# Three engines' orders written by hand from the output projection on, in a one-layer mLSTM and attention encoder

## The chip, the cores and the metric

The kernel runs on one core of a Trainium2 chip. A core has engines that run beside each other and wait for one another through semaphores: TensorE (PE) multiplies matrices into PSUM, VectorE (DVE) and ScalarE (ACT) work elementwise, GpSimd (POOL) and SyncE (SP) here mostly issue DMAs. The metric is the device time of one execution in microseconds (us); lower is better. Times are medians of several executions; the profile is of one more.

## What is computed

One layer on a sequence of 512 rows of width 2048, all in float32, with two branches (an mLSTM and a differential attention), their gated mix, an output projection and a feed-forward block:

```python
def reference(x, ..., w_out, norm2_w, w_ffn_in, w_ffn_out, final_norm_w):
    ...                                   # branches, gates -> mix  (512 x 2048)
    x = x + mix @ w_out                   # output projection    "wo"
    h = _rmsnorm(x, norm2_w)
    u = h @ w_ffn_in                      # 2048 x 11264         "fi"
    x = x + gated(u) @ w_ffn_out          # 5632 x 2048          "fo"
    return _rmsnorm(x, final_norm_w)
```

The change touches what begins with `mix @ w_out`. (The last four lines are condensed; `gated` is the silu-gated half product of the feed-forward block.)

## The kernel before

**One product.** A float32 product is made of three passes with reduced operands: each operand is split into a high part and a rest, and `mm3` (L145) issues high x high, high x low and low x high. The high part is an ACT copy (`whi_...`, L149), the low part a DVE subtraction (`wlo_...`, L150). So each piece of weights (128x1024) costs ACT one copy and DVE one subtraction before TensorE can use it, and so does each piece of activations, called a factor here (`..h`, `..l`, two halves of 128x512).

**Seven instead of eight.** `seven` multiplies 2x2 blocks with seven products (Strassen's scheme in Winograd's form). Each product Q1, Q5, Q6, Q2, Q3, Q7, Q4 takes a sum of weight blocks and a sum of activation blocks. The sums of weights are DVE additions: raw_b += raw_a (L348), `t2` (L356), raw_e += raw_f (L362), `t2` += raw_d (L369). A chunk runs over groups g of 512 rows: Q1, Q5, Q6 for every group, then Q2, Q3, Q7, then Q4. A product of one group is twelve matmuls of 128x512. Names say all this: `wlo_fi4_Q12` is the low part of the weights of chunk fi4, product Q1, group 2. The last chunks, fo, also have four plain products, `W12`, `W22`, `W11`, `W21`.

**Chunks.** wo0 and wo1 (4 groups each), fi0 to fi10 (4 groups, 28 products each), fo0 and fo1 (10 groups and the plain ones). While a chunk runs, `post` takes finished PSUM banks into tiles: in wo and fo by `added` (L802 to L837: the residual is added by an accumulating DMA that POOL issues, the squares for the norm are ACT's), in fi by L938 to L956 (sigmoid on ACT, sums and gate on DVE).

**Between chunks.** `turned` transposes a finished block on TensorE (eight transposes of 128x128 make a set, `T`), ACT copies them out of PSUM (`fg_X`, `h_X`), and four DVE operations, `sum_` at L863 (S1, then X21, X11 and X12 in place), make the sums of activation blocks for later products; SP stores each sum, and ACT's queue stores the plain blocks. `h2c` are the blocks after wo (h20 and h21 from wo0), `fg_j` those after fi chunk j. They come back from DRAM as `fs` (L988, POOL's queue) and are split into factors while fo runs. A set of transposes of chunk j runs inside chunk j+1.

**What sets the order.** The code hands over instructions in the order in which it is written; a scheduler then orders each engine's own stream by priorities and by times that it estimates, and puts the waits in. `take` (L206) fetches the weight pieces of product n and has piece n+2 made (`AHEAD` = 2). `work` (L332) does one queued factor after each product; `later` (L213) puts a step off by a number of nanoseconds of a clock that counts matmuls. Each engine then runs its stream in order, and an instruction that waits holds what stands behind it on its engine.

## Time and profile before

| | us |
|---|---|
| median of 3 runs | 2681.12 (2680.89 to 2682.58) |
| the profiled execution | 2683.64 |
| its span | 2681.9 |
| TensorE busy in the span | 2605.4 (97%) |
| VectorE busy | 2129.2 (79%) |
| ScalarE busy | 1312.8 (49%) |

The span is the time from the first to the last instruction of the profiled execution; the time itself holds 1.74 us more around it. Shares of the whole span are means over stages. By the names in the timeline of TensorE, wo lasts from 1177.6 to 1358.2 us, fi to 2225.1, fo to 2670.9, and the end to 2681.9. The granted clock is a share of TensorE's full clock of 2.4 GHz, so 0.50 is its lower level, 1.2 GHz.

### The profile page before, as it was taken

To read this page: it belongs to the slowest core of one execution; us is meant where nothing else is said; L and a number is where in the kernel's file an instruction comes from. 1 tells how busy PE (TensorE), PEld (TensorE's weight loads), DVE (VectorE), ACT (ScalarE), POOL (GpSimd) and SP (SyncE) were. 2 spreads that over 40 slices of the span, in tenths; PEclk is the share of its full clock that TensorE was granted. 3 is DMA by queue.
4 is the path that set the end of the run, shared out by engine and by line. 5 is a ranking of instruction groups with operands and counts; after the bars stand their busy time and mean duration, and the time that the engine had idled before them with its cause. 6 is when DMAs were issued, how large, how long until landed. Compare 5 with 4: busy or idle time off the path is not lost.

```text
span 2681.9 us, 33178 instructions
## 1 busy us (share of the span) xinstructions
PE 2605.4 (97%) x12136; PEld 2160.3 (81%) x12136; DVE 2129.2 (79%) x2692; ACT 1312.8 (49%) x1848; POOL 254.9 (10%) x448
## 2 busy tenths in 40 slices
PE   8999999999999999999899999999999999999997
PEld 7888888877878998887778888888888878777876
DVE  8977788777877676596788888888888889888885
ACT  8544444444544463345464444444444446546654
POOL 1000000011110113101110000000000002222211
PEclk9999999989999999999999999999999999999999
DMA  7655666633432346437665555555555578777763
GB/s 263 233 186 185 201 200 216 223 103 116 123 110 71 115 134 241 175 130 233 223 199 183 194 165 181 195 192 186 175 199 173 181 284 286 252 249 257 242 220 94
DMA packets 162227, 508.97 MB, mean 190 GB/s; under 512 B 21832, under 2 KB 22120, under 8 KB 162064
## 3 DMA queue, kind: packets, MB, share of 16 engines
q1 hardware_dynamic: 111456, 379.77, 41.3%
q0 software_dynamic: 33712, 97.71, 12.1%
q10 hardware_dynamic: 16896, 29.37, 3.1%
q8 instruction: 95, 1.56, 0.2%
q14 instruction: 68, 0.56, 0.1%
HBM read 445.41 MB, written 50.87 MB: 185 GB/s over the span
## 4 chain that ended last, share of the span: by engine, by line
PE 71%; DVE 12%; issue 7%; DMA 7%; ACT 2%; POOL 1%; SPq 0%; DVEq 0%; POOLq 0%; ACTq 0%
PE fi_b L145 12%; PE fi_c L145 8%; PE fi_a L145 8%; PE fo_b L145 4%; PE aqk_b L145 3%; PE fo_c L145 3%; PE fo_a L145 3%; PE mqk_b L145 3%; PE mv_p L145 3%; PE ba_p L145 3%; PE bm_p L145 3%; PE ga_b L145 2%; PE gm_b L145 2%; PE gm_a L145 1%; PE gm_c L145 1%
## 5 line engine op out<-in xcount | busy, mean ns | idle before, releaser
L145 PE MATMUL aqk_b<-xs,whi_aqk 128*128 128x512 f32 x512 | 162.0, 396 | 0.0
L149 ACT CAST whi_fi_Q<-fi_Q_t 128x1024 fp32r<-128x1024 f32 x88 | 92.5, 1052 | 117.7 <-PE fi_b L145 97.7
L145 PE MATMUL fi_a<-whi_fi_Q,h_X 128*128 128x512 f32 x440 | 147.0, 391 | 0.0
L145 PE MATMUL fi_c<-whi_fi_Q,h_S 128*128 128x512 f32 x440 | 145.0, 390 | 0.0
L145 PE MATMUL fi_b<-whi_fi_Q,h_S 128*128 128x512 f32 x352 | 115.5, 389 | 0.0
L145 PEld LDWEIGHTS aqk_b<-xs,whi_aqk 128*128 128x128 f32 x512 | 97.1, 191 | 19.6
L150 DVE TENSOR_TENSOR wlo_fi_Q<-fi_Q_t,whi_fi_Q 128x1024 fp32r<-128x1024 f32 x88 | 106.5, 1220 | 5.5 <-ACT whi_fi_Q L149 5.3
L145 PE MATMUL aqk_b<-xs,wlo_aqk 128*128 128x512 f32 x256 | 100.8, 394 | 0.0
L145 PEld LDWEIGHTS fi_c<-whi_fi_Q,h_S 128*128 128x128 f32 x440 | 83.0, 189 | 17.3
L145 PEld LDWEIGHTS fi_a<-whi_fi_Q,h_X 128*128 128x128 f32 x440 | 82.6, 188 | 16.8
L362 DVE TENSOR_TENSOR raw_fi_e<-raw_fi_e,raw_fi_f 128x1024 f32<-128x1024 f32 x44 | 53.9, 1224 | 52.6 <-DMA raw_fi_e<-in_w_ffi 52.6
L988 POOL DMA_DIRECT2D fs_X<-fg_X11d x22 | 11.9, 539 | 830.5 <-DVE wlo_fi_Q L150 785.3
L145 PE MATMUL fi_a<-wlo_fi_Q,h_X 128*128 128x512 f32 x220 | 85.9, 390 | 0.6 <-DVE wlo_fi_Q L150 0.6
L145 PE MATMUL fi_c<-wlo_fi_Q,h_S 128*128 128x512 f32 x220 | 85.8, 390 | 0.0
L348 DVE TENSOR_TENSOR raw_fi_b<-raw_fi_b,raw_fi_a 128x1024 f32<-128x1024 f32 x44 | 53.8, 1224 | 36.0 <-DMA raw_fi_b<-in_w_ffi 33.6
L149 ACT CAST whi_fi_Q<-raw_fi_e 128x1024 fp32r<-128x1024 f32 x44 | 46.4, 1055 | 72.6 <-PE fi_b L145 51.4
L145 PE MATMUL ba_p<-whi_ba,hahl 128*128 128x512 f32 x256 | 81.8, 390 | 0.0
L145 PE MATMUL mqk_b<-xs,whi_mqk 128*128 128x512 f32 x256 | 80.9, 396 | 0.0
L145 PE MATMUL bm_p<-whi_bm,hmhl 128*128 128x512 f32 x256 | 80.5, 391 | 0.0
L149 ACT CAST whi_fi_Q<-raw_fi_b 128x1024 fp32r<-128x1024 f32 x44 | 46.5, 1057 | 68.8 <-PE fi_c L145 52.1
L149 ACT CAST whi_fi_Q<-raw_fi_f 128x1024 fp32r<-128x1024 f32 x44 | 46.5, 1056 | 68.3 <-PE fi_c L145 63.9
L145 PEld LDWEIGHTS fi_b<-whi_fi_Q,h_S 128*128 128x128 f32 x352 | 66.1, 188 | 13.7
(843 smaller groups left out, 8479.5 us busy)
## 6 DMA issues: line engine op xcount, KB each, us to landing
raw_fi_a<-in_w_ffi SPq DMA_DIRECT2D x44, 512.0 KB, 3.4
raw_fi_b<-in_w_ffi SPq DMA_DIRECT2D x44, 512.0 KB, 4.2
raw_fi_c<-in_w_ffi SPq DMA_DIRECT2D x44, 512.0 KB, 4.1
raw_fi_d<-in_w_ffi SPq DMA_DIRECT2D x44, 512.0 KB, 4.2
raw_fi_f<-in_w_ffi SPq DMA_DIRECT2D x44, 512.0 KB, 3.5
raw_fi_e<-in_w_ffi SPq DMA_DIRECT2D x44, 512.0 KB, 3.6
raw_aqk<-in_w_aqk SPq DMA_DIRECT2D x32, 512.0 KB, 3.5
raw_fo_a<-in_w_ffo SPq DMA_DIRECT2D x20, 512.0 KB, 4.5
```

Source lines behind the costliest of these rows:

```text
L145: T.matmul(dst, lhs[l], rhs[r], start=first and i == 0, stop=last and i == 2, skip_group_check=skip)
L149: A.copy(hi, src)
L150: V.tensor_tensor(lo, src, hi.bitcast(F32), ALU.subtract)
L348: V.tensor_tensor(raws[r12], raws[r12], raws[r11], ALU.add)
L362: V.tensor_tensor(raws[r12], raws[r12], raws[r22], ALU.add)
L988: G.dma_start(got[n], fgd[g][f_].rearrange("p (k c) -> p k c", k=2))
```

## The change

From the first product of wo0 on, `tc.manual_schedule()` is entered and never left: each engine then issues in the order in which the code is written, and the scheduler moves nothing. Along with it the code is written in another order:

- `parts` makes the high part of a weight piece at once, when `issue` comes to it, and hands back a function that makes the low part. `take(n)` has the high part of piece n+2 made as before, and calls the functions so that low parts up to piece n+1 are made.
- `post` of a finished product is not called behind that product but put off by 2000 ns (`behindhand`), that is about one product.
- `factor` makes the high part at once and puts the low part into a list; `work` takes one of the list each time. `flush` empties it before the two sums that change a tile whose low part is still to be made.
- The factors of fo are made only when fewer than five of those made are unused (`used`), instead of whenever `work` comes by.

```diff
@@ -174,9 +174,13 @@
...
-        lo = wpool.tile([P, n], F32R, tag="lo", name=f"wlo_{name}")
-        split(src, hi, lo)
-        return tuple(w.rearrange("p (k c) -> p k c", k=kt) for w in (hi, lo))
+        A.copy(hi, src)
+
+        def low():
+            lo = wpool.tile([P, n], F32R, tag="lo", name=f"wlo_{name}")
+            V.tensor_tensor(lo, src, hi.bitcast(F32), ALU.subtract)
+            return tuple(w.rearrange("p (k c) -> p k c", k=kt) for w in (hi, lo))
+        return low
...
@@ -197,6 +201,22 @@
+    region = []
+
+    def written():
+        if not region:
+            region.append(ctx.enter_context(tc.manual_schedule()))
+
+    def behindhand(fn):
+        if region:
+            later(2000, fn)
+        else:
+            fn()
+
+    lows = [0]
...
@@ -206,6 +226,9 @@
         issue(n + AHEAD)
+        while lows[0] < min(len(ready), n + (2 if region else 3)):
+            ready[lows[0]] = ready[lows[0]]()
+            lows[0] += 1
...
     def work(must=False):
+        if low_parts:
+            low_parts.pop(0)()
...
         def body(nm, it):
+            if nm == "wo0":
+                written()
...
+                used[0] += len({(g, f_) for _, f_ in to} - met)
+                met |= {(g, f_) for _, f_ in to}
...
-                    post(q_, bank)
+                    behindhand(lambda q_=q_: post(q_, bank))
...
@@ -457,8 +490,19 @@
-        split(src, *w)
-        out[f_] = w
+        A.copy(w[0], src)
+
+        def low():
+            V.tensor_tensor(w[1], src, w[0].bitcast(F32), ALU.subtract)
+            out[f_] = w
+        if region:
+            low_parts.append(low)
+        else:
+            low()
+
+    def flush():
+        while low_parts:
+            low_parts.pop(0)()
...
         def s2():
+            flush()
...
         def s4():
+            flush()
...
             if q_ == "Q4" and j == NFB - 1:
+                used[0] = -4
                 stream()
...
-        when(lambda: True, [lambda n=n: make(n) for n in range(len(need))])
+        for n in range(len(need)):
+            when(lambda n=n: n < used[0] + 5, [lambda n=n: make(n)])
```

Nothing is added or left out: on every engine the program holds the same instructions as before, and up to wo0 in the same order. Three places show the moves.

DVE, in chunk fi4. TensorE's products run Q10, Q50, Q60, Q11, Q51, Q61, Q12, Q52 and so on; a set of transposes for `fg3` stands in the middle of Q11 before the change. Before:

```order
L150 TENSOR_TENSOR wlo_fi4_Q61_14745<-fi4_Q61_t2_14742,whi_fi4_Q61_14744 128x1024
L863 TENSOR_TENSOR fg3_S1_14769<-fg3_X21_14759,fg3_X22_14766 128x512
L356 TENSOR_TENSOR fi4_Q63_t2_14880<-raw_fi4_b3_14721,raw_fi4_c3_14740 128x1024
L863 TENSOR_TENSOR fg3_X21_14759<-fg3_X11_14619,fg3_X21_14759 128x512
L150 TENSOR_TENSOR wlo_fi4_Q12_14787<-raw_fi4_a2_14630,whi_fi4_Q12_14786 128x1024
L863 TENSOR_TENSOR fg3_X11_14619<-fg3_S1_14769,fg3_X11_14619 128x512
L369 TENSOR_TENSOR fi4_Q60_t2_14685<-fi4_Q60_t2_14685,raw_fi4_d0_14784 128x1024
L863 TENSOR_TENSOR fg3_X12_14627<-fg3_X12_14627,fg3_X11_14619 128x512
```

After, at the same place; the set of transposes now stands in the middle of Q51:

```order
L181 TENSOR_TENSOR wlo_fi4_Q61_14764<-fi4_Q61_t2_14742,whi_fi4_Q61_14744 128x1024
L909 TENSOR_TENSOR fg3_S1_14787<-fg3_X21_14777,fg3_X22_14784 128x512
L909 TENSOR_TENSOR fg3_X21_14777<-fg3_X11_14637,fg3_X21_14777 128x512
L909 TENSOR_TENSOR fg3_X11_14637<-fg3_S1_14787,fg3_X11_14637 128x512
L909 TENSOR_TENSOR fg3_X12_14645<-fg3_X12_14645,fg3_X11_14637 128x512
L376 TENSOR_TENSOR raw_fi4_b2_14648<-raw_fi4_b2_14648,raw_fi4_a2_14614 128x1024
L181 TENSOR_TENSOR wlo_fi4_Q12_14807<-raw_fi4_a2_14614,whi_fi4_Q12_14762 128x1024
L384 TENSOR_TENSOR fi4_Q62_t2_14823<-raw_fi4_b2_14648,raw_fi4_c2_14673 128x1024
```

The four sums, which wait for the transposes, stand in one piece ahead of the addition and of `wlo` of Q12, where `wlo` of Q12 had two of them behind it. The addition to raw_b2, made much earlier before, stands between too. The same holds at fi1 to fi10, ten times.

DVE, from wo0 into wo1 (h21 and h20 are the blocks made of wo0's result; `wo0_x210` and `wo0_x211` are its last tiles). Before:

```order
L348 TENSOR_TENSOR raw_wo1_b2_11451<-raw_wo1_b2_11451,raw_wo1_a2_11410 128x1024
L150 TENSOR_TENSOR wlo_wo1_Q10_11413<-raw_wo1_a0_11194,whi_wo1_Q10_11412 128x1024
L150 TENSOR_TENSOR wlo_wo1_Q50_11455<-raw_wo1_b0_11213,whi_wo1_Q50_11454 128x1024
L837 TENSOR_TENSOR wo0_x210_11064<-wo0_x210_11064,wo0_b0_10807 128x512
L863 TENSOR_TENSOR h21_S1_11482<-h21_X21_11433,h21_X22_11441 128x512
L837 TENSOR_TENSOR wo0_x211_11071<-wo0_x211_11071,wo0_b1_10808 128x512
L863 TENSOR_TENSOR h21_X21_11433<-h21_X11_11469,h21_X21_11433 128x512
```

After:

```order
L376 TENSOR_TENSOR raw_wo1_b0_11213<-raw_wo1_b0_11213,raw_wo1_a0_11194 128x1024
L181 TENSOR_TENSOR wlo_wo1_Q10_11433<-raw_wo1_a0_11194,whi_wo1_Q10_11406 128x1024
L384 TENSOR_TENSOR wo1_Q60_t2_11478<-raw_wo1_b0_11213,raw_wo1_c0_11231 128x1024
L181 TENSOR_TENSOR wlo_wo1_Q50_11482<-raw_wo1_b0_11213,whi_wo1_Q50_11431 128x1024
L909 TENSOR_TENSOR h21_S1_11508<-h21_X21_11452,h21_X22_11460 128x512
L909 TENSOR_TENSOR h21_X21_11452<-h21_X11_11495,h21_X21_11452 128x512
L909 TENSOR_TENSOR h21_X11_11495<-h21_S1_11508,h21_X11_11495 128x512
L909 TENSOR_TENSOR h21_X12_11504<-h21_X12_11504,h21_X11_11495 128x512
L883 TENSOR_TENSOR wo0_x210_11083<-wo0_x210_11083,wo0_b0_10809 128x512
L883 TENSOR_TENSOR wo0_x211_11090<-wo0_x211_11090,wo0_b1_10810 128x512
L181 TENSOR_TENSOR wlo_wo1_Q60_11535<-wo1_Q60_t2_11478,whi_wo1_Q60_11480 128x1024
```

The addition for group 2 no longer stands ahead of `wlo` of Q10; the last two tiles of wo0, which TensorE needs for the next set of transposes, stand behind all four sums of h21.

DVE, near the end, in fo1 (`fnw` is the final norm's weight, `ss1` and `pw_in` lead to POOL's reciprocal root, L1056 to L1065 are the norm of half the rows). Before:

```order
L834 TENSOR_TENSOR fo1_x110_21596<-fo1_x110_21596,fo1_a0_20847 128x512
L150 TENSOR_TENSOR fs1_6_X22l_22421<-fs6_X22_22334,fs1_6_X22h_22420 128x512
L834 TENSOR_TENSOR fo1_x111_21599<-fo1_x111_21599,fo1_a1_20848 128x512
L150 TENSOR_TENSOR fs1_7_X22l_22445<-fs7_X22_22356,fs1_7_X22h_22444 128x512
L150 TENSOR_TENSOR fs1_8_X22l_22465<-fs8_X22_22378,fs1_8_X22h_22464 128x512
L150 TENSOR_TENSOR wlo_fo1_Q42_22559<-fo1_Q62_t2_21011,whi_fo1_Q42_22558 128x1024
L150 TENSOR_TENSOR fs1_9_X22l_22481<-fs9_X22_22398,fs1_9_X22h_22480 128x512
L1008 TENSOR_TENSOR fo1_x220_21556<-fo1_x220_21556,fnw3_20611 128x512
```

After:

```order
L1056 TENSOR_TENSOR fo1_x121_21571<-fo1_x121_21571,fnw3_20579 128x512
L880 TENSOR_TENSOR fo1_x110_21601<-fo1_x110_21601,fo1_a0_20822 128x512
L1060 TENSOR_REDUCE ss1_22521<-ss3p_231 128x1
L589 TENSOR_SCALAR pw_in_22524<-ss1_22521 128x1
L1067 TENSOR_SCALAR fo1_x120_21564<-fo1_x120_21564,rstd3_22523 128x512
L1065 SCALAR_TENSOR_TENSOR fo1_x110_21601<-fo1_x110_21601,rstd3_22523,fnw2_20578 128x512
L880 TENSOR_TENSOR fo1_x111_21604<-fo1_x111_21604,fo1_a1_20823 128x512
L1060 TENSOR_REDUCE ss1_22538<-ss3p_231 128x1
L589 TENSOR_SCALAR pw_in_22541<-ss1_22538 128x1
L1067 TENSOR_SCALAR fo1_x121_21571<-fo1_x121_21571,rstd3_22540 128x512
L1065 SCALAR_TENSOR_TENSOR fo1_x111_21604<-fo1_x111_21604,rstd3_22540,fnw2_20578 128x512
L181 TENSOR_TENSOR wlo_fo1_Q42_22559<-fo1_Q62_t2_20992,whi_fo1_Q42_22490 128x1024
```

`wlo` of Q42 stood ahead of that norm, and stands behind it now; and the second tile, `fo1_x111`, is added only when the first one is through. The tiles `x210` and `x211` behind the last product follow each other in the same way.

## Rows read from the trace of the kernel before

**Rows 1.** the page: the chain that ended last, shares of the span by engine

```profile
PE 71%; DVE 12%; issue 7%; DMA 7%; ACT 2%; POOL 1%; SPq 0%; DVEq 0%; POOLq 0%; ACTq 0%
```

**Rows 2.** busy time (count) of each engine by stretch, granted clock, DMA share, GB/s

```profile
1170.00:1248.00 78.00, 77.45 (x348) 63.41 (x347) 64.39 (x72) 37.69 (x46) 5.29 (x7) 1.00 0.54 169
1248.00:1300.00 52.00, 45.51 (x193) 36.26 (x193) 34.59 (x36) 25.27 (x47) 5.74 (x10) 0.90 0.72 243
1300.00:1340.00 40.00, 36.22 (x154) 28.34 (x153) 31.00 (x34) 21.26 (x29) 9.52 (x16) 1.00 0.71 238
1340.00:1368.00 28.00, 24.77 (x115) 19.70 (x115) 19.76 (x24) 18.95 (x41) 9.11 (x14) 0.94 0.76 220
1368.00:2140.00 772.00, 771.75 (x3478) 639.31 (x3477) 647.55 (x670) 355.56 (x390) 1.33 (x3) 1.00 0.54 183
2140.00:2226.00 86.00, 83.70 (x373) 68.16 (x372) 72.07 (x74) 38.30 (x43) 7.43 (x14) 1.00 0.77 278
2300.00:2460.00 160.00, 153.63 (x662) 122.86 (x661) 132.39 (x152) 90.47 (x129) 39.28 (x69) 1.00 0.80 265
2460.00:2600.00 140.00, 137.47 (x602) 112.14 (x601) 124.58 (x135) 80.55 (x104) 28.75 (x52) 1.00 0.76 253
```

**Rows 3.** timelines, fi4: start, length, engine, line, operation; PE, ACT, then DVE

```profile
1683.78 0.39 PE L145 MATMUL fi_a<-whi_fi_Q,h_X 128*128 128x512 f32 x1
...
1685.15 1.03 PE L849 MATMUL fg_T<-ident,fv 128*128 128x128 f32 x8
...
1687.39 0.39 PE L145 MATMUL fi_c<-whi_fi_Q,h_S 128*128 128x512 f32 x1
...
1685.78 1.08 ACT L854 COPY fg_X<-fg_T 128x512 f32<-128x512 f32 x2 [0.70 <-PE fg_T L849]
...
1687.38 0.68 DVE L863 TENSOR_TENSOR fg_S<-fg_X,fg_X 128x512 f32<-128x512 f32 x1
1687.98 1.22 DVE L356 TENSOR_TENSOR fi_Q_t<-raw_fi_b,raw_fi_c 128x1024 f32<-128x1024 f32 x1
1689.11 0.69 DVE L863 TENSOR_TENSOR fg_X<-fg_X,fg_X 128x512 f32<-128x512 f32 x1
```

**Rows 4.** timelines, wo0 into wo1: DVE, PE, and ScalarE's DMA queue

```profile
1261.02 1.23 DVE L348 TENSOR_TENSOR raw_wo_b<-raw_wo_b,raw_wo_a 128x1024 f32<-128x1024 f32 x1 [6.92 <-DMA raw_wo_b<-in_w_out]
...
1270.36 0.69 DVE L863 TENSOR_TENSOR h_X<-h_X,h_X 128x512 f32<-128x512 f32 x1 [0.57 <-DMA h_X12d<-h_X]
...
1279.08 0.80 PE L145 MATMUL wo_a<-wlo_wo_Q,mix_X 128*128 128x512 f32 x1 [3.25 <-DVE wlo_wo_Q L150]
...
1265.21 0.33 ACTq L860 DMA_DIRECT2D h_X12d<-h_X  x1
```

**Rows 5.** two stretches by busy time, as in rows 2

```profile
1280.00:1285.00 5.00, 5.00 (x13) 3.84 (x13) 3.90 (x5) 1.04 (x1) 0.00 (x0) 0.50 0.93 282
1314.00:1323.00 9.00, 5.50 (x20) 3.75 (x21) 6.64 (x9) 6.65 (x12) 0.00 (x0) 1.00 0.78 297
```

**Rows 6.** waits of DVE, whole span: waited for, us in total, times, longest

```profile
DVE raw_fi_b L348 <- DMA raw_fi_b<-in_w_ffi: 33.6, 21, 4.6
...
DVE wlo_fo_Q L150 <- ACT whi_fo_Q L149: 21.1, 19, 8.6
```

**Rows 7.** the page: DMA issues, KB each and us to landing

```profile
raw_fi_b<-in_w_ffi SPq DMA_DIRECT2D x44, 512.0 KB, 4.2
```

**Rows 8.** timelines of the end: ACT, DVE, then PE

```profile
2641.19 0.63 ACT L1004 ACTIVATE x2j<-fo_x 128x512 f32<-128x512 f32 x1 [0.81 <-PE fo_b L145]
...
2644.40 0.16 DVE L1012 TENSOR_REDUCE ss<-ss3p 128x1 f32<-128x4 f32 x1
...
2646.50 0.15 DVE L1012 TENSOR_REDUCE ss<-ss3p 128x1 f32<-128x4 f32 x1
...
2670.91 1.37 DVE L837 TENSOR_TENSOR fo_x<-fo_x,fo_b 128x512 f32<-128x512 f32 x2 [5.17 <-PE fo_b L145]
...
2650.36 1.12 PE L145 MATMUL fo_b<-whi_fo_Q,fs_X22h 128*128 128x512 f32 x2 [3.54 <-ACT whi_fo_Q L149]
```

More of the change, by code (lines that the diff above doesn't have):

```diff
@@ L324, in build @@
     behind = []
+    used = [0]
+    low_parts = []
     def work(must=False):
+        if low_parts:
+            low_parts.pop(0)()
         if behind:
@@ L414, in body @@
             begun = set()
+            met = set()
             for n, (q_, g, to, posts) in enumerate(seq):
```

## The prediction

> **What bounds the kernel now.** I read the chain that ended last first: TensorE holds 71% of it and VectorE 12% [rows 1]. Then the stretches one by one, because the mean hides them: in the long stretch of fi, TensorE is busy 771.75 of 772 us [rows 2], so there nothing waits and nothing can be won. What can be won stands at the ends: the stretches in which TensorE's busy time is below the stretch, or its granted clock below 1.00 [rows 2]. I count the loss of a stretch as its length less TensorE's busy time, plus, where the clock is down, half of the time at the lower level (a mean of 0.90 over 52 us is 10.4 us at half speed, so 5.2 lost). That gives, in us: 1170 to 1248, 0.55; 1248 to 1300, 6.5 and 5.2, so 11.7; 1300 to 1340, 3.8; 1340 to 1368, 3.2 and 1.7, so 4.9; 2140 to 2226, 2.3; 2300 to 2460, 6.4; 2460 to 2600, 2.5 [rows 2]. At the end TensorE waits once for 3.54 us [rows 8].
>
> Why TensorE waits there is seen in the timelines: VectorE stands at an instruction that the scheduler put ahead of a low part. From wo0 into wo1 it stood 6.92 us at an addition whose load had not landed, with the low part that TensorE needed behind it, and TensorE waited 3.25 us in the next such case [rows 4]. In fo the low parts themselves come late: VectorE waited up to 8.6 us for a high part which ACT had not made [rows 6]. The change takes such jumps away, and puts others in.
>
> **The change, part by part.** The instructions are the same on every engine, so no busy time is added or saved. Only waits move. The sums below are of TensorE's time, since it is the engine that sets the end.
>
> *Ten crossings from one fi chunk to the next (loss).* This is the largest new term, and it falls in the stretch that loses nothing now. Call s the start of product Q51, which now holds the transposes in its middle. Six matmuls take 1.37 us (1683.78 to 1685.15 [rows 3]), so 0.228 each and 2.74 for a product; with the transposes a product took 3.61 (to 1687.39 [rows 3]). ACT's two copies end 1.71 us after the transposes begin (1685.78 plus 1.08 [rows 3]), so at s+3.08, and the sums can begin at about s+3.13. A sum of 128x512 is followed by the next instruction after 0.60 us (1687.38 to 1687.98 [rows 3]); these four depend on one another, so each costs between 0.60 and its length of 0.69 and a little, 0.70. Together 2.4 to 2.8 us. The addition behind them takes 1.13 (1687.98 to 1689.11 [rows 3]), and the low part of Q12, of the same shape, 1.22 until it is whole. It is there at s+7.9 to s+8.3. TensorE asks for it after Q51 (3.61), Q61 (2.74) and one matmul with the high part (0.23): at s+6.58. It waits 1.3 to 1.7 us, ten times: 13 to 17 us, and I take 15. Now the same sums lie between low parts and additions that were made early, so that nothing is late.
>
> [...]
>
> *fo (gain).* For three products VectorE now has three low parts, two additions and three low parts of factors, 5 times 1.13 and 3 times 0.60 [rows 3], so 7.45 of TensorE's 8.22 us, in a fixed round. Low parts are made a product ahead, which covers the blocks of additions for finished products except one at the head of fo1 (six of them in one place, some 3.6 us). I expect 1 us left there. What goes is 8.9 us by the stretches [rows 2], and about 2.5 more that they hide: a matmul's record lasts 0.39 where the next starts after 0.228 [rows 3], so each wait hides 0.16, and I count some sixteen. Gain 10.5, between 6 and 12.
>
> *wo0 into wo1 (small loss).* Two standings of VectorE go, and two come. First: h21's last sums write over blocks that ACT's queue is still storing; one such store lasted from 1265.21 to 1270.36, 5.15 us [rows 4]. Counted from the start of Q10, the transposes, copies and that store let the sums through at about +9.3, the two tiles behind them are ready at +10.5, and TensorE wants them at its transposes after Q50, at +6.3. It waits 4.2 us; for each us that a store takes longer, one more. Second: the sums of h20 and an addition stand ahead of the low part of Q11, as at the fi crossings, where 1.3 to 1.7 came out, but with four shorter copies and two squares on ACT before them, some 2 to 3 us more: 3.4 to 5. And the clock: waits of this size were followed by the lower level, 0.50 granted from 1280 to 1285, where 13 matmuls stand and 22 would fit [rows 5], so 2 us each time. Together 10 to 17, I take 13, against 11.7 now: loss 1.5, between a gain of 2 and a loss of 5.
>
> *Smaller gains.* 1300 to 1340: the waits come from factors that stand ahead of weight pieces, which the new order holds back; 3.8 now [rows 2], 1 left, gain 3 (0 to 3.5). wo1 into fi0: the last tiles of wo1 stand ahead of the addition that waits for its load; 4.9 now, about 0.5 left, gain 4.5 (3 to 5). End of fi: 2.3 now, 0.7 left, gain 1.5. Start of wo: gain 0.5.
>
> *The end (loss).* The low part of Q42 moves behind a norm of half the rows. From the first square (2641.19 now [rows 8]) there follow, all in one line: four squares at 0.63, a multiplication and an addition (0.60 each), a square and its sum (0.82), a round of reduction, POOL's root and scaling (2.10, from 2644.40 to 2646.50 [rows 8]), an addition, a square, another round, and the low part: 2.5 + 1.2 + 0.8 + 2.1 + 0.65 + 0.8 + 2.1 + 1.2, so 11.4. The squares begin, by the order, behind the high part of Q42, 1.25 to 2.5 us after Q40 (an estimate: a copy of 128x1024 and its wait, or the place where they began now), and TensorE wants Q42 two products and one matmul after it, at 5.7. It waits 7 to 8, against 3.54 at Q43 now [rows 8]. Behind TensorE's end the two last tiles go through the norm one after the other instead of side by side (two additions in 1.37 us now [rows 8]): an addition and a square more, 1.5. Loss 5.5, between 4 and 7.
>
> Sum: -15 + 10.5 - 1.5 + 3 + 4.5 + 1.5 + 0.5 - 5.5 = -2, so 2 us longer. Against the profiled execution of 2683.64 that is 2685.6; the median of the runs shown lies 2.5 below it, so 2683. The measurement can tell about 0.2%, 5.4 us, so this is no change that can be told. With every term at its better end the sum is a gain of 9, at its worse end a loss of 20.
>
> **The rivals.**
>
> *The crossings in fi cost nothing (faster).* If the low part of Q12 is in time after all, the 15 us go: 2668. For it: VectorE has slack in fi (647.55 of 772 [rows 2]). Against it: the slack lies elsewhere, the line from the copies to the low part has no gap in it, and nothing in the order lets the low part pass the sums. Chance 0.10.
>
> *The crossing into wo1 comes cheap (faster).* If the stores land within 2 us, the first wait is 1 instead of 4.2, and without a long wait the clock may stay up: 6 instead of 13, and with fo at its better end the sum is a gain of 6.5, 2674.5. For it: the store that took 5.15 us [rows 4] ran beside loads at a DMA share of 0.72 [rows 2]. Against it: the same loads run now. Chance 0.20.
>
> *Additions stand before late loads (slower).* Each addition now stands right ahead of a low part that is due a product later, where it was made several products early. VectorE waited 21 times for raw_fi_b, 33.6 us in all, 1.6 each [rows 6], and none of it reached TensorE. If one such wait in each of the eleven fi chunks does, that is 17.6 us: 2701. For it: VectorE can no longer do other work meanwhile. Against it: these loads land in 4.2 us [rows 7] and are issued more than three products ahead; it decides from a landing of about 10 us. Chance 0.15.
>
> *The clock falls at every crossing (slower).* Waits of 1.5 us might each bring a stretch at half speed, 2 us by the row from 1280 [rows 5], ten times: 2703. Against it: from 1314 to 1323 TensorE was busy only 5.50 of 9 us and the granted clock stayed at 1.00 [rows 5]. The page "TensorE: Matmul & The Clock Gate" of the Trainium skill, section "A second HAM failure mode: psum-queue depth-cycling", says that short idling between groups of matmuls, when frequent enough, lets the clock swing between its levels; these rows don't show it, though crossings are 78 us apart (28 products of 2.74 and two sets of transposes of 0.87) and none of this kind is in the trace. Chance 0.05.
>
> *The order doesn't bite.* If the instructions kept their order, the time would be 2681. The listing shows them moved. Chance 0.02.
>
> **How the numbers follow.** The forecast, 2683, has the rest, 0.48, and its own spread is about 7 us to either side. Faster by over 0.2% is below 2675.8: 0.10, of the cheap crossing 0.12, of the forecast 0.10, so 0.32. Slower is above 2686.5: 0.15, 0.05 and of the forecast 0.15, so 0.35. Within is 0.33. The range leaves out most of the late loads and of the clock's case above and a little below: 2668 to 2698.
>
> **What would show it.** In the profile after: ten waits of TensorE of 1.3 to 1.7 us for a low part of fi, one in each chunk from fi1, at Q12; from 2300 to 2600 TensorE busy to within 2 us of the stretch; a wait of 7 us in fo1's Q4 and 12.5 us behind the last matmul; a granted clock of 1.00 all through fi. I am wrong if TensorE's busy time in fi is still whole, if VectorE waits for loads of raw_fi_b and TensorE for what stands behind, or if TensorE's clock is down in fi.

## The result, and the profile after

The changed kernel takes 2705.46 us (median of four runs, 2704.85 to 2710.97) against 2681.01 for the kernel before: a ratio of 1.0099, 95% interval 1.0081 to 1.0117. It is slower, by 24 us, and outside the range forecast. The profiled execution has a span of 2703.4 us against 2681.9, so 21.5 us can be traced.

Where they lie is told by the first matmul of each stage in the two timelines (the end counts from VectorE's first addition there), beside what the terms of the sum add up to. Read this way, fi of the kernel before lasts to 2225.3 us and not to 2225.1.

| stage | before, us | after, us | change | forecast |
|---|---|---|---|---|
| up to the first matmul of wo | 1177.6 | 1173.7 | -3.9 | 0 |
| wo | 180.6 | 175.1 | -5.5 | -6.5 |
| fi | 867.1 | 898.7 | +31.6 | +13.5 |
| fo | 445.6 | 443.7 | -1.9 | -6.5 |
| behind the last matmul | 11.0 | 12.2 | +1.2 | +1.5 |

wo and the end came out near the forecast. fi did not, and a part of fo's gain is missing. The first row is no effect of the change: up to wo every engine has the same order, and the profiled executions of the changed kernel and of the versions of it below take between 1171.1 and 1184.0 us there. The stretches of the kernel after (columns as in rows 2) answer to those of before:

```profile
1248.00:1300.00 52.00, 45.41 (x201) 37.08 (x200) 36.50 (x38) 27.48 (x47) 5.51 (x9) 0.93 0.66 224
1300.00:1340.00 40.00, 36.02 (x152) 29.13 (x151) 31.17 (x35) 19.88 (x27) 9.66 (x17) 0.96 0.82 258
1340.00:1368.00 28.00, 28.00 (x141) 23.39 (x140) 22.08 (x24) 20.52 (x42) 4.15 (x8) 1.00 0.64 219
1368.00:2140.00 772.00, 744.90 (x3321) 608.55 (x3320) 632.35 (x643) 339.52 (x371) 1.04 (x1) 1.00 0.52 178
...
2236.00:2270.00 34.00, 30.97 (x131) 24.87 (x130) 28.70 (x34) 19.49 (x28) 6.01 (x12) 0.90 0.58 204
...
2300.00:2640.00 340.00, 337.53 (x1487) 278.60 (x1487) 304.06 (x335) 197.78 (x268) 72.09 (x129) 1.00 0.74 251
```

From 1368 to 2140 TensorE was busy 771.75 of 772 us [rows 2]; now it is 744.90, at a granted clock that stays at 1.00. So 27 us of waits came into a stretch that had next to none. From 2300 to 2640, in fo, TensorE now idles 2.5 us, where it idled 8.9 (6.4 and 2.5 [rows 2]), so the gain that the sum put there came. But at the head of fo, 2236 to 2270, it idles 3.0 us and its clock is down to a mean of 0.90.

The waits of TensorE (waited for, us in total, times, longest) say for what:

```profile
PE fi_a L145 <- DVE wlo_fi_Q L181: 15.8, 10, 1.6
PE fi_b L145 <- DVE wlo_fi_Q L181: 12.8, 12, 1.5
PE fo_b L145 <- DVE wlo_fo_Q L181: 11.6, 4, 7.5
```

Ten waits for a low part by bank a of fi, 1.6 us each, are the forecast ones, at Q12. Twelve by bank b, 12.8 us, were not forecast: ten of them stand at Q60, one in each crossing, and two in fi0.

One crossing, from fi3 into fi4, by its three engines. TensorE's timeline (start, length, engine, line, operation, in brackets the idle time before and its releaser):

```profile
1600.35 0.39 PE L145 MATMUL fi_b<-whi_fi_Q,h_S 128*128 128x512 f32 x1
1601.77 0.50 PE L145 MATMUL fi_b<-wlo_fi_Q,h_S 128*128 128x512 f32 x1 [1.03 <-DVE wlo_fi_Q L181]
...
1615.42 0.50 PE L145 MATMUL fi_a<-wlo_fi_Q,h_X 128*128 128x512 f32 x1 [1.58 <-DVE wlo_fi_Q L181]
```

The high part of Q60 runs at 1600.35, the low part would at 1600.57 and starts at 1601.77. Then the low part of Q12 is 1.58 us late. VectorE's timeline:

```profile
1594.98 1.23 DVE L181 TENSOR_TENSOR wlo_fi_Q<-raw_fi_b,whi_fi_Q 128x1024 fp32r<-128x1024 f32 x1 [1.83 <-ACT whi_fi_Q L177]
1596.12 0.68 DVE L1000 TENSOR_TENSOR fv<-fi_b,fv 128x512 f32<-128x512 f32 x1
...
1599.88 0.69 DVE L975 TENSOR_TENSOR fv<-fv,fs 128x512 f32<-128x512 f32 x1
1600.49 1.22 DVE L181 TENSOR_TENSOR wlo_fi_Q<-fi_Q_t,whi_fi_Q 128x1024 fp32r<-128x1024 f32 x1
...
1610.23 0.69 DVE L909 TENSOR_TENSOR fg_S<-fg_X,fg_X 128x512 f32<-128x512 f32 x1 [2.69 <-ACT fg_X L900]
1610.95 0.69 DVE L909 TENSOR_TENSOR fg_X<-fg_X,fg_X 128x512 f32<-128x512 f32 x1
```

From 1596.12 to 1600.49 it runs the six operations that finish Q4 (the first and the last are shown), in one piece of 4.37 us, and only then the low part of Q60, which is whole at 1601.71. Ahead of them it had stood 1.83 us at the low part of Q50, for its high part. The sums begin at 1610.23 and follow each other by 0.72. ACT shows why that high part is late:

```profile
1591.93 0.59 ACT L900 COPY fg_X<-fg_T 128x512 f32<-128x512 f32 x1 [2.50 <-PE fg_T L895]
1592.55 0.33 ACTq L906 DMA_DIRECT2D fg_X11d<-fg_X  x1
1592.92 0.59 ACT L900 COPY fg_X<-fg_T 128x512 f32<-128x512 f32 x1 [0.40 <-ACT fg_X L900]
...
1593.90 1.05 ACT L177 CAST whi_fi_Q<-raw_fi_b 128x1024 fp32r<-128x1024 f32 x1 [0.40 <-ACT fg_X L900]
```

It stands 2.50 us for the transposes, makes a copy, issues its store, stands 0.40, makes the second copy, issues its store, stands 0.40, and only then makes the high part of Q50.

Each crossing has a third, small wait, at the low part of Q42 in the old chunk, here in the next crossing:

```profile
1669.73 0.39 PE L145 MATMUL fi_b<-whi_fi_Q,h_X22h 128*128 128x512 f32 x1
1670.21 0.50 PE L145 MATMUL fi_b<-wlo_fi_Q,h_X22h 128*128 128x512 f32 x1
```

The low part starts 0.48 us behind the high part, where a matmul follows another after 0.23. The block ahead of it is VectorE's four operations that finish Q2, 2.8 us long (1584.62 to 1587.40 at the crossing above). Counted from start to start, and with the slower matmul behind each, a crossing loses 0.37 us at Q42, 1.3 at Q60 and 1.85 at Q12, so 3.5, and ten of them 35.

The end, TensorE and then VectorE:

```profile
2668.27 0.80 PE L145 MATMUL fo_b<-wlo_fo_Q,fs_X22h 128*128 128x512 f32 x1 [7.49 <-DVE wlo_fo_Q L181]
```

```profile
2656.89 2.53 DVE L1056 TENSOR_TENSOR fo_x<-fo_x,fnw 128x512 f32<-128x512 f32 x4 [4.88 <-ACT x2j L1052]
...
2666.99 1.22 DVE L181 TENSOR_TENSOR wlo_fo_Q<-fo_Q_t,whi_fo_Q 128x1024 fp32r<-128x1024 f32 x1
...
2691.18 0.69 DVE L883 TENSOR_TENSOR fo_x<-fo_x,fo_b 128x512 f32<-128x512 f32 x1 [5.17 <-PE fo_b L145]
...
2694.74 0.68 DVE L883 TENSOR_TENSOR fo_x<-fo_x,fo_b 128x512 f32<-128x512 f32 x1
```

The final norm of two tiles runs in line from 2656.89 to 2666.99, then comes the low part of Q42, and TensorE has waited 7.49 us, against 3.54 before [rows 8]. Behind the last matmul the second tile is added at 2694.74, 3.56 us after the first; before, both additions took 1.37 us together [rows 8].

### The profile page after: what moved, and what is told of

Read it like the earlier page. It is cut to its first block, busy times and chain, and to the rows that moved or that the text cites. A ratio compares the mean times of both kernels' runs of the same rounds, so it can differ in the third digit from the quotient of the medians.

```text
span 2703.4 us, 33161 instructions
## 1 busy us (share of the span) xinstructions
PE 2604.4 (96%) x12136; PEld 2159.3 (80%) x12136; DVE 2142.5 (79%) x2692; ACT 1313.5 (49%) x1848; POOL 253.5 (9%) x448
## 4 chain that ended last, share of the span: by engine, by line
PE 73%; DVE 13%; issue 6%; ACT 3%; DMA 2%; POOL 1%; ACTq 0%; DVEq 0%; POOLq 0%; SPq 0%
PE fi_b L145 9%; PE fi_a L145 8%; PE fi_c L145 7%; PE fo_b L145 6%; PE fo_a L145 4%; PE fo_c L145 4%; PE bm_p L145 3%; PE aqk_b L145 3%; PE mqk_b L145 3%; PE mv_p L145 3%; PE ba_p L145 3%; PE ga_b L145 2%; DVE wlo_fi_Q L181 2%; PE gm_b L145 2%; PE wo_b L145 2%
## 5 line engine op out<-in xcount | busy, mean ns | idle before, releaser
L181 DVE TENSOR_TENSOR wlo_fi_Q<-fi_Q_t,whi_fi_Q 128x1024 fp32r<-128x1024 f32 x88 | 106.7, 1222 | 10.2 <-ACT whi_fi_Q L177 9.2
L145 PE MATMUL fi_a<-wlo_fi_Q,h_X 128*128 128x512 f32 x220 | 86.8, 394 | 15.8 <-DVE wlo_fi_Q L181 15.8
L181 DVE TENSOR_TENSOR wlo_fi_Q<-raw_fi_d,whi_fi_Q 128x1024 fp32r<-128x1024 f32 x44 | 53.8, 1224 | 44.5 <-ACT whi_fi_Q L177 44.4
L145 PE MATMUL fi_b<-wlo_fi_Q,h_S 128*128 128x512 f32 x176 | 69.8, 397 | 11.3 <-DVE wlo_fi_Q L181 11.3
L177 ACT CAST whi_fi_Q<-raw_fi_d 128x1024 fp32r<-128x1024 f32 x44 | 46.4, 1054 | 68.9 <-PE fi_a L145 50.0
L145 PEld LDWEIGHTS fi_b<-whi_fi_Q,h_S 128*128 128x128 f32 x352 | 66.1, 188 | 13.5
```

Of the source, the lines that this page charges most:

```text
L145: T.matmul(dst, lhs[l], rhs[r], start=first and i == 0, stop=last and i == 2, skip_group_check=skip)
L177: A.copy(hi, src)
L181: V.tensor_tensor(lo, src, hi.bitcast(F32), ALU.subtract)
```

## The experiments

Each run has the kernel before beside it on its own chip, so times are told as differences to that: the change itself is 24.4 us behind it. The stretch from 1368 to 2140 us is the same as in rows 2; the changed kernel idles 27.1 us in it. The intervals of the ratios are 4 to 6 us wide to either side, and the untouched part ahead of wo alone differs by up to 13 us from one profiled execution to another. The length of fi in the profile is steadier: 867.1 us before, 898.7 in the change, and 898.9 in each of the two runs that leave fi alone (the steps, the seven factors). So where fi is what a run changes, its length is told too.

**The sums, one product later** (`sums` makes the four additions).

```diff
+            if nm.startswith("fg"):
+                later(2000, sums)
```

> The changed kernel with one thing moved: the four sums after the transposes of an fi chunk are put off by 2000 ns, about one product, so that the low part of Q12 stands ahead of them. Theory (two separate waits at each crossing in fi, the sums ahead of the low part of Q12 and the finished-product additions ahead of the low part of Q60): TensorE's ten waits for the low part of Q12 go (15.8 us idle and some 1.7 hidden), those for Q60 stay at 1.0 us each; the new place delays the low part of Q52 by at most 0.4 us each. So 13 to 17 us less than 2705: 2688 to 2692. Rival 1 (VectorE simply has too little time around a crossing, whatever stands first): the wait moves on to the low part of Q52 and the time stays within 4 us of 2705. Rival 2 (what costs is that every engine issues in written order, all through): no change in the other waits, and less than 5 us of gain.

Measured: ratio 1.0035 (1.0019 to 1.0052), 2690.25 us, 10.1 behind the kernel before, so 14.3 gained. fi takes 879.9 us, 18.8 less than in the change.

```profile
1368.00:2140.00 772.00, 759.11 (x3395) 623.02 (x3394) 646.68 (x658) 347.39 (x380) 1.04 (x1) 1.00 0.55 182
```

TensorE idles 12.9 us in the stretch, 14.2 less. The waits for Q12 are gone, and no new one stands at Q52. The first half of the theory holds, both rivals fall.

**Low parts one product earlier.** The number of pieces with low parts, undone.

```diff
-        while lows[0] < min(len(ready), n + (2 if region else 3)):
+        while lows[0] < min(len(ready), n + 3):
```

> The changed kernel with its own number of low parts undone: in the written region too the low parts are made up to piece n+2, one product earlier than in the change. Theory: the low part of Q60 then stands ahead of the additions for the finished Q4, and the low part of Q12 ahead of the sums, so both waits of each crossing go, some 29 us, and the wait of 3.1 us at the head of fo0 with its half-speed stretch (5 us); what VectorE loses is only standing for a high part, about 1 us per product, where it has room. So 2705 less 28 to 35: 2670 to 2677, below the kernel before. Rival 1 (too little time around a crossing): the waits move to Q51 or Q52 and at least half of the 29 us stays, 2690 or more. Rival 2 (standing for high parts costs VectorE the time it needs, above all in fo, where it has 7.5 us of work in 8.2): fo gets 10 us longer or more, and the time is 2680 to 2690.

Measured: ratio 1.0562 (1.0538 to 1.0585), 2831.21 us. This is 126 us worse than the change, where 28 to 35 better was expected. Rival 2 named standing for high parts, but for fo alone, and had a time below 2705: by the profile fo is 59 us longer than in the change, and fi 51. VectorE's waits (columns as above), first of this kernel and then of the changed one:

```profile
DVE wlo_fi_Q L181 <- ACT whi_fi_Q L177: 207.4, 186, 4.7
DVE wlo_fo_Q L181 <- ACT whi_fo_Q L177: 107.7, 79, 5.8
```

```profile
DVE wlo_fi_Q L181 <- ACT whi_fi_Q L177: 107.2, 132, 2.2
DVE wlo_fo_Q L181 <- ACT whi_fo_Q L177: 28.6, 38, 3.0
```

VectorE stands 207 us in fi instead of 107, and 108 in fo instead of 29. What ACT itself waits for most, ahead of fi's high parts, again in this kernel and in the changed one:

```profile
ACT whi_fi_Q L177 <- DVE raw_fi_e L390: 149.2, 44, 4.9
```

```profile
ACT whi_fi_Q L177 <- PE fi_b L145: 125.7, 88, 1.7
```

In the change ACT waits for TensorE to free a tile. Here it waits for VectorE's own addition of the same piece: addition, high part and low part of a piece follow each other from VectorE to ACT and back, and the low part, right behind in the order, holds all that follows. So the change's later low parts are not what costs; they are what makes a written order bearable.

**The new code, ordered by the scheduler.**

```diff
-            region.append(ctx.enter_context(tc.manual_schedule()))
+            region.append(True)
```

> The changed kernel without the manual schedule: the code is written in the new order, with everything put off as in the change, but the scheduler orders each engine. Theory (the loss comes from where the written order puts single blocks, so a scheduler that lets low parts pass takes it away in fi, and brings its own waits back in wo and fo): fi within 12 us of the kernel before, wo and fo within 8 of it, so 2672 to 2692. Rival (the new code order itself, low parts and additions a product later, costs the time whoever orders): 2700 or more, with waits of TensorE at the crossings in fi.

Measured: ratio 1.0135 (1.0116 to 1.0154), 2716.26 us, 36 behind the kernel before. The rival is right: the new code costs whoever orders it, and the written order is the better of the two by some 12 us. fi alone takes 902.1 us, 35 more than before, where the theory allowed 12. Its waits by TensorE:

```profile
PE fi_b L145 <- DVE wlo_fi_Q L181: 18.7, 27, 2.6
...
PE fi_a L145 <- DVE wlo_fi_Q L181: 4.9, 4, 3.4
```

They are other waits than those of the written order, more of them and shorter in the mean, with four left at bank a instead of ten. So the loss in fi doesn't hang on the manual schedule alone; the moves below show which instructions stand in the way in the written order, and what stands in the way under the scheduler is left open.

**The final norm in steps** (`root` is the reduction and POOL's root, `scaled` the scaling and the stores).

```diff
-                later(0 if n else 30000, lambda: V.tensor_tensor(x, x, env["fnw"][c], ALU.mult))
+                later(2600 if n else 30000, lambda: V.tensor_tensor(x, x, env["fnw"][c], ALU.mult))
...
+            later(2600, root)
+            later(5200, scaled)
```

> The changed kernel with the final norm of fo1 cut in three steps, each put off by one product: additions and squares, then sums and roots, then scaling; so low parts stand between the steps, and at the end both rows of a pair go through side by side. Theory (the end loses by its order): the wait of 7.5 us at Q42 goes, with the half-speed stretch behind it (2 us), and 1.2 us behind the last matmul, so 9 to 11 us less: 2694 to 2697, all of it behind 2655 us of the span. Rival (POOL's root and ACT's squares are the bound there): at least 4 us of the wait stay.

Measured: ratio 1.0075 (1.0052 to 1.0098), 2699.49 us, 19.4 behind, so 5.0 gained; its runs spread from 2689.1 to 2702.8, more than the others', and the profile is of the shortest. The stage shows the gain better: fo lasts from 2244.3 to 2676.4, 432.1 us against 443.8.

```profile
2656.90 0.15 DVE L1063 TENSOR_REDUCE ss<-ss3p 128x1 f32<-128x4 f32 x1
...
2657.16 0.15 DVE L1063 TENSOR_REDUCE ss<-ss3p 128x1 f32<-128x4 f32 x1
...
2658.06 1.22 DVE L181 TENSOR_TENSOR wlo_fo_Q<-fo_Q_t,whi_fo_Q 128x1024 fp32r<-128x1024 f32 x1
...
2676.38 1.37 DVE L883 TENSOR_TENSOR fo_x<-fo_x,fo_b 128x512 f32<-128x512 f32 x2 [5.17 <-PE fo_b L145]
```

The reductions of both tiles stand side by side, a low part follows at 2658.06, and behind the last matmul both additions take 1.37 us again. Of the 11.7 us that fo is shorter, some 3.4 are not the edit's: at the head of fo TensorE waits 2.9 us as in the change, but the granted clock stays at 1.00 from 2236 to 2270, where it was 0.90. The rest, 8.3, and the 1.2 behind the last matmul make 9.5, so the theory (9 to 11) holds by the stage, while the timed gain is half of it and not settled closer than that.

**The Q4 additions, split** (`last` has the three operations of one tile).

```diff
+                    def last(i=i):
...
+                    if i:
+                        later(2600, last)
+                    else:
+                        last()
```

> The changed kernel with one thing moved: of the six VectorE operations that finish an fi chunk's Q4, the three of the second tile are put off by one more product, so that only three stand ahead of the low part of Q60. Theory (the other half of each crossing is these six operations, 4.4 us in a row, ahead of the low part of Q60): the ten waits of TensorE for the low part of Q60 go (1.0 us idle each, 1.2 from start to start), and the eleventh, at the head of fo0, shrinks from 3.3 us to under 1.5, with its half-speed stretch; the waits for Q12 stay at 1.6 each. So 12 to 17 us less than 2705: 2688 to 2693. Rival (the high part of Q50 is what is late, behind ACT's copies and its two stores): the waits for Q60 stay above 0.7 each and the gain is under 5.

Measured: ratio 1.0065 (1.0048 to 1.0081), 2700.28 us, 17.2 behind, so 7.2 gained where 12 to 17 was expected. fi takes 889.7 us, 8.9 less than in the change.

```profile
1368.00:2140.00 772.00, 753.04 (x3356) 615.03 (x3355) 640.67 (x652) 344.49 (x377) 1.04 (x1) 1.00 0.54 180
```

TensorE idles 19.0 us, 8.1 less. The waits for Q60 are gone, but 0.3 us from start to start stays at Q51 (a piece of additions is now between), and at the head of fo the wait has only moved: bank c waits up to 2.0 us there. The theory holds for the place and not for the whole of the price.

**Three moves at once**, the sums, the split and the steps.

> The changed kernel with the sums put off by 2000 ns, the Q4 additions of an fi chunk split over two products and fo1's final norm in three steps. Theory (three separate places, whose costs add): 15 (measured for the sums) and 12 to 17 and 9 to 12 less than 2705, so 2661 to 2669, that is 0.4% to 0.8% below the kernel before; fi's loss is then within 6 us of the kernel before. Rival (the waits at a crossing share one cause, too little VectorE time there, and moving both blocks brings a wait back at Q11, Q51 or Q52): 2675 or more.

Measured: ratio 0.9959 (0.9943 to 0.9975), 2670.06 us, 13.0 ahead of the kernel before and 37 ahead of the change. The expected gain on the kernel before, 0.4% to 0.8%, is met at its low end.

```profile
1368.00:2140.00 772.00, 766.92 (x3428) 629.71 (x3427) 650.46 (x663) 350.86 (x383) 1.04 (x1) 1.00 0.55 181
```

TensorE idles 5.1 us in the stretch. The two moves in fi, 14.2 and 8.1, make 22.3 apart and 22.0 together, and by the length of fi (871.1) 18.8 and 8.9 make 27.7 apart and 27.6 together. So the two waits of a crossing have two causes. The rival falls.

**Finished products at once.** The putting off, undone.

```diff
         if region:
-            later(2000, fn)
+            fn()
```

> The changed kernel with one part undone: finished products are taken out of PSUM right behind the product, not one product later. Theory (a block of additions costs what stands behind it): the six operations of an fi chunk's Q4 then stand ahead of the low part of Q50, begin with the last matmul of Q4 and are through some 5.6 us after it, where TensorE wants Q50 after 3.0; so ten waits of 2 to 3 us in place of 1.2, and more at the other finished products: 2715 to 2740. Rival (putting them off is what costs): below 2697.

Measured, one run: 2759.69 us, 77 behind. The direction is right and the size was 20 us too small.

```profile
1368.00:2140.00 772.00, 724.50 (x3142) 587.66 (x3141) 603.41 (x612) 323.19 (x354) 1.04 (x1) 0.98 0.51 167
```

```profile
PE fi_c L145 <- DVE wlo_fi_Q L181: 33.6, 11, 3.3
PE fi_b L145 <- DVE wlo_fi_Q L181: 19.4, 22, 2.5
```

Eleven waits of up to 3.3 us stand at Q50 (bank c), as expected, and twenty-two more by bank b. And the granted clock is down to a mean of 0.98 over the 772 us, some 15 us, which the expectation had not counted: with waits this long TensorE does fall to half speed in fi.

**The manual schedule alone**, entered in the kernel before.

> The kernel before with nothing but the manual schedule, entered at the same place: low parts two products ahead and right behind their high parts, finished products at once, factors whenever there is room. Theory (in written order VectorE stands for each high part, as where low parts were made a product earlier, which gave 2831; and the blocks of additions stand ahead of low parts): 2830 to 2890. Rival (the written order is good by itself, and the moved low parts and additions are what costs): 2700 or less.

Measured, one run: 2869.51 us, 186 behind. VectorE stands as in the run with earlier low parts:

```profile
DVE wlo_fi_Q L150 <- ACT whi_fi_Q L149: 219.0, 178, 4.1
```

So 186 us are the price of the written order for the old code. Undone singly at the change, the later low parts are worth 126 us and the late additions 52; together with the change's other edits they take 162 of the 186 away (less than 126 and 52, so the two overlap), and 24 stay.

**The first transposes of a chunk, one product earlier.**

```diff
-                later(5000, lambda: turned(f"fg{j}", u2, 0, X, 0, fgd[j]))
+                later(2400, lambda: turned(f"fg{j}", u2, 0, X, 0, fgd[j]))
```

> The changed kernel with the first set of transposes of each fi chunk put off by 2400 ns instead of 5000, so that it stands one product earlier, and ACT's two copies and two stores stand ahead of the high part of the next chunk's Q10 instead of Q50. Theory as it is now (the six operations alone would be just in time, 0.1 us late at most; what makes the low part of Q60 late is that they begin late, since VectorE first stands 1.8 us for the high part of Q50, which ACT makes behind those copies and stores): the waits for Q60 fall from 1.0 to under 0.3 each, without any other move, so 9 to 14 us less than 2705: 2691 to 2696. Rival (the length of the six operations is the cause, whenever they begin): the waits for Q60 stay above 0.7 each and the time stays within 4 us of 2705.

Measured: ratio 1.0082 (1.0060 to 1.0103), 2698.31 us, 22.4 behind, so 2.0 gained by the time, not clear of the uncertainty. fi takes 890.6 us, 8.1 less than in the change. TensorE and VectorE at the same crossing:

```profile
1603.63 0.50 PE L145 MATMUL fi_b<-wlo_fi_Q,h_S 128*128 128x512 f32 x1 [0.65 <-DVE wlo_fi_Q L181]
...
1596.85 1.22 DVE L181 TENSOR_TENSOR wlo_fi_Q<-raw_fi_b,whi_fi_Q 128x1024 fp32r<-128x1024 f32 x1
1597.99 0.68 DVE L1000 TENSOR_TENSOR fv<-fi_b,fv 128x512 f32<-128x512 f32 x1
```

The wait is 0.65 us, between the two bounds. VectorE no longer stands at Q50's low part, but at the one before it, that of Q10, for 1.05 us: the high part of Q10 is the late one now, and the line of low parts behind it lets the six operations begin only 0.37 us earlier, counted from the time at which TensorE wants Q60. The small wait at Q42 is gone too, which with the shorter wait at Q60 makes most of the 8 us of fi. Neither expectation holds as it stands.

**Stores by POOL.**

```diff
-                nc.scalar.dma_start(keep[f_].rearrange("p (k c) -> p k c", k=2), out[f_])
+                (G if nm.startswith("fg") else nc.scalar).dma_start(keep[f_].rearrange("p (k c) -> p k c", k=2), out[f_])
```

> The changed kernel with the stores of the plain fi blocks issued by POOL instead of ACT. ACT stands 0.40 us at each of them after a copy. Theory (the high part of Q50 is late by ACT's wait for the transposes, its two copies and two stores): two of the stores stand ahead of it, so it comes 0.7 to 0.8 us earlier and the wait for the low part of Q60 falls by as much, from 1.0 to 0.2 to 0.4 each; the copies for the sums come 0.4 earlier, so the wait for Q12 is at most 0.4 shorter. 7 to 12 us less than 2705: 2693 to 2698. Rival (the stores cost nothing, ACT would wait for the transposes anyway): within 3 us of 2705.

Measured: ratio 1.0072 (1.0055 to 1.0089), 2695.28 us, 19.4 behind, so 5.0 gained; 7 to 12 was expected. fi takes 890.1 us, 8.6 less than in the change, which is within what was expected. TensorE, VectorE and ACT:

```profile
1602.57 0.50 PE L145 MATMUL fi_b<-wlo_fi_Q,h_S 128*128 128x512 f32 x1 [0.19 <-DVE wlo_fi_Q L181]
...
1616.22 0.50 PE L145 MATMUL fi_a<-wlo_fi_Q,h_X 128*128 128x512 f32 x1 [1.58 <-DVE wlo_fi_Q L181]
...
1595.64 1.23 DVE L181 TENSOR_TENSOR wlo_fi_Q<-raw_fi_b,whi_fi_Q 128x1024 fp32r<-128x1024 f32 x1 [0.83 <-ACT whi_fi_Q L177]
1596.78 0.68 DVE L1000 TENSOR_TENSOR fv<-fi_b,fv 128x512 f32<-128x512 f32 x1
...
1593.58 1.07 ACT L900 COPY fg_X<-fg_T 128x512 f32<-128x512 f32 x2 [2.50 <-PE fg_T L895]
```

The wait for Q60 is 0.19 us, as expected, and that for Q12 still 1.58. VectorE stands 0.83 us for the high part of Q50 and begins the six operations 1.0 us earlier against TensorE's need. This separates the two parts of the cause. The six operations and the low part need 4.37 and 1.22, so 5.6 us, and between the end of Q4 and the low part of Q60 lie two products and one matmul, 5.7: that alone would be just in time. What made it late is the start, by ACT's copies and stores. Either way out takes the wait away, a start on time here or a shorter block in the split.

**Seven factors ahead instead of five.**

```diff
-            when(lambda n=n: n < used[0] + 5, [lambda n=n: make(n)])
+            when(lambda n=n: n < used[0] + 7, [lambda n=n: make(n)])
```

> The changed kernel with the factors of fo held to seven ahead instead of five (more than seven can't be held, there are not enough tiles). Theory (in written order VectorE's round in fo, three low parts, two additions and three halves of factors for three products, is the same whatever the lead; the hold only bounds the tiles): from 2300 to 2640 TensorE loses under 5 us as in the changed kernel, 3.3 there. Rival (factors that run ahead take VectorE's time from the low parts, as the scheduler let them, and the hold is what made fo faster): 8 us lost or more.

Measured, one run: 2711.36 us. From 2300 to 2640:

```profile
2300.00:2640.00 340.00, 337.53 (x1486) 278.48 (x1485) 305.99 (x337) 198.52 (x269) 72.71 (x131) 1.00 0.74 255
```

The changed kernel has 337.53 there too. Whether five or seven are held is nothing to fo, as the theory says. Whether it needs a hold at all isn't shown: larger ones were not tried, since the tiles don't suffice. (The end lost some 3.5 us more, 1.5 at the low part of Q42 and 2.1 at one of a plain product, in one run.)

**Five moves**: the three, the earlier transposes, and the sums after wo0 put off too.

```diff
+            later(2000 if nm.startswith("fg") else 6000, sums)
```

> The kernel with the three moves (sums of fi later, Q4 additions split, final norm in steps) and two more: the first set of transposes one product earlier as in the run of this name, and the sums after wo0 put off by 6000 ns, so that the last two tiles of wo0 and two low parts stand ahead of them. Theory (each place where a block that waits stands ahead of a low part costs by itself): from 2666 (the span with three moves) the 4.2 us wait at the transposes after wo0 and the 2.8 us wait at Q11 go with their half-speed stretch, 7 to 11 us, and the 3 us and the half-speed stretch at the head of fo0, 3 us: a span of 2653 to 2658 and a median of 2656 to 2662, 0.8% below the kernel before. Rival (VectorE has no room there, and the waits move on, to wo1's Q51 and Q12): within 4 us of the kernel with three moves.

Measured: ratio 0.9914 (0.9898 to 0.9931), 2653.66 us, 22 ahead of the kernel before and 47 ahead of the change; a little better than expected.

```profile
1248.00:1300.00 52.00, 50.09 (x236) 41.19 (x235) 40.49 (x41) 29.05 (x50) 8.26 (x14) 1.00 0.79 266
1368.00:2140.00 772.00, 770.58 (x3469) 637.32 (x3470) 656.55 (x670) 355.09 (x387) 1.86 (x3) 1.00 0.53 184
```

TensorE idles 1.9 us from 1248 to 1300, where it idled 6.6 in the change and 6.5 before, at a clock of 1.00 instead of 0.93; and 1.4 us in the long stretch of fi. fi takes 862.3 us, 4.8 less than before. At the head of fo, bank c still waits 2.0 us with half speed behind it, so that part of the theory didn't come. This version beats both kernels.

## Why the prediction was wrong, point by point

**The crossings in fi.** This is the step that failed. The term, 15 us, was right as far as it went: ten waits at Q12, 15.8 us idle and 0.16 hidden in each, so 17.4; taking the sums away from there gave back 14 by the time, and 18.8 by the length of fi. What failed is that the part on the crossings names only this place. It takes the order from the sums on and does not follow what stands between Q4's last matmul and the low part of Q60. There the same rule holds, a block ahead of a low part, with six operations and a low part in a space of 5.7 us, and the row of ACT that makes them late (two stores that each hold ACT for 0.40 us between copy and copy). That is ten waits of 1.03 us idle, 1.2 from start to start, and an eleventh at the head of fo with half a clock behind it, 3.0 us idle and 10% of the clock over 34 us. The block that finishes Q2, ahead of the low part of Q42, is a third such place, 0.37 each. So a crossing loses 3.5 us where 1.5 was forecast. The sentence on fo, that low parts made a product ahead cover the additions for finished products, is the step in words: it was worked out for fo's additions of 0.60 and not for fi's Q4.

**fo.** Gain 10.5 forecast. The kernel before, in 340 us of fo:

```profile
2280.00:2620.00 340.00, 331.09 (x1438) 268.12 (x1438) 290.65 (x322) 192.99 (x261) 71.79 (x128) 1.00 0.73 242
```

It runs 1438 matmuls there, and the changed kernel 1487 in 340 us from 2300 on: 49 more, which at 0.227 each is 11 us. So the term was right. The head of fo, unforeseen, took some 6 of it back, of which 3.4 are the clock, and the end 4.

**wo.** Forecast 6.5 shorter, measured 5.5, with some luck, since the split was off both ways: from 1248 to 1300 6.6 us idle and 3.6 by the clock, 10.2 where I took 13, because the second wait was 2.3 us and not 3.4 to 5 (the first was 4.2, as forecast); from 1300 to 1340 nothing was won, but 1.8 lost (4.0 idle and 1.6 by the clock, 3.8 before), since ACT stands 8.6 us for a load there; from 1340 to 1368 the gain of 4.9 came whole.

**The end.** Forecast 5.5, measured 4.0 more of waiting (7.49 against 3.54) and 1.2 behind the last matmul: 5.2.

**The rivals.** None was right. The loads were not late: the waits of TensorE that count are for low parts behind sums and additions, and moving those took them away. The clock did not fall at the crossings: granted 1.00 over the 772 us with some twenty waits of 1.0 to 1.6. So the rule of the Trainium skill's page "TensorE: Matmul & The Clock Gate", section "A second HAM failure mode: psum-queue depth-cycling", on short idling is not what this trace shows. The waits of 2.9 us at the head of fo and of 7.49 us were followed by half speed, and the rival's mechanism is real at longer waits: with finished products at once, waits of up to 3.3 us brought the clock of the same stretch to 0.98. The result was slower by a mechanism that I had priced at one place and had not looked for at the next. The signs that I had named came, or nearly (waits at Q12 of 1.6 us, fo busy to within 2.5 us, 7.49 us in fo1's Q4 and 12.2 behind, a clock of 1.00 in fi), so they could not tell of the other place.

## What to carry to other kernels

In a written order a block costs what stands behind it, so go through every item that another engine will want at a given time (here the low parts of weights) and add up what stands ahead of it back to the last event that it waits for, at every place where a block stands, not only at the one that the diff shows. An instruction that waits for another engine belongs one period behind its releaser in such an order: the same order with low parts right behind their high parts was 126 us slower. And put long blocks in pieces between the items that are due: three such moves turned a loss of 24 us into a gain of 13, five into 22.

## What the runs showed of the hardware that I had not expected

A store issued from ACT's own queue behind a copy holds ACT 0.40 us before its next copy (0.40 idle at 1592.92, with the store at 1592.55); with the stores on POOL's queue the two copies follow each other in one piece of 1.07 us. Additions that depend on each other follow by 0.72 us (1610.23, 1610.95), against 0.60 for independent ones [rows 3], which is above the upper bound of 0.70 that I used. And the same wait does not always cost the same clock: TensorE idles 2.94 us for the same low part at the head of fo in the change and in three of its versions; in the change and with seven factors the granted clock fell behind it (0.90 and 0.95 from 2236 to 2270), with the sums later and with the steps it stayed at 1.00.
